# Expert weights in 16 KB runs over nine places, and the last two experts as one unit with a split tail

## The chip, the cores and the metric

The kernel runs on one core of a Trainium2 chip. The metric is device microseconds of one execution, the median of several runs. The kernel before takes 1447.01 us (three runs, 1445.4 to 1449.87). TensorE is called PE in the profile, VectorE DVE, ScalarE ACT, GpSimd POOL and SyncE SP.

## The reference

One layer over 256 latent and 256 context tokens of width 1024. A first part (modulated norm, a wide input projection, a bidirectional mLSTM, differential attention, gates, an output projection) gives the stream x of 256 x 1024. The change lies in what follows:

```
logits = u @ router_w + router_b                 # 256 tokens, 32 experts
top_val, top_idx = top_k(logits, 4); gate = softmax(top_val)
per expert e:   h   = u[tok] @ w1[e] + b1[e]                     # w1[e]: 1024 x 2048, 8 MiB
                act = min(h_glu,7) * sigmoid(1.702 min(h_glu,7)) * (clip(h_lin,-7,7) + 1)
                y   = act @ w2[e] + b2[e]                        # w2[e]: 1024 x 1024, 4 MiB
x = x + g2 * sum over the chosen experts of gate * y
out = rmsnorm(x, final_norm_g)
```

Everything is float32. The weights of the 32 experts are 384 MiB, and all of them are read in each execution.

## The kernel before, in words

**Experts.** Each expert has room for 64 tokens (CAP). Experts are worked off in pairs (loop at L1122). Tokens of a pair are picked with one-hot matmuls (`gather`, L1023), `expert` (L1051) multiplies them with the eight 1 MiB pieces of w1 (L1056), DVE and ACT make the activation (L1061 to L1065), a callback `between` does work of the neighbouring pair, four transposes and a copy give the activation transposed (L1069, L1071), and four 1 MiB pieces of w2 follow (L1078). `evac_y` (L1082) scales the result by g2, and `scatter` (L1088) adds it to x1 with four matmuls and four DVE adds. The scatter of a pair runs inside the next pair's first `between`; the last pair's scatter stands alone (L1159).

**Weights.** `epiece` (L1001) asks for the next 1 MiB piece of 128 partitions x 8 KB, in program order on SP's queue. The places are the 21 of ORDER (L36): two of a pool of their own (`spare`), four of the pool `ring` that the first part uses too, and 15 in memory that the first part frees piece by piece. A place is filled again when the matmuls that read it are done; SP waits in order, so one place that isn't free holds back all later loads.

**End.** After the last scatter stands an If (L1163) for the case that an expert has more than 64 tokens; its body is not entered with these inputs. Behind it come the final norm (sums of squares on ACT and DVE, L1201 to L1206; the reciprocal root by eight small DVE operations, L121 to L130; scaling on POOL, ACT and DVE, L1211 to L1215) and four output stores from SP (L1216).

Of the kernel before, what the change touches and what calls it, by code (L numbers as in the profile page):

```python
# [10 lines left out]
F32 = mybir.dt.float32  # L11
# [3 lines left out]
AF = mybir.ActivationFunctionType  # L15
OP = mybir.AluOpType
# [4 lines left out]
D = 1024  # L21
# [3 lines left out]
E = 32  # L25
# [1 line left out]
EPS = 1e-6  # L27
LAM_INIT = 0.2
NEG = -1.0e30
R1, R2, R3, LOOK = 4, 15, 2, 2  # L30
PER_M, PER_D = 5, 5
FAR = 4096.0

HOMES = dict(xc=[0], wk=[1, 2], mk=[3], mv=[4, 5], sums=[6, 7], hm=[8], dk=[1, 3], dv=[2, 4], og=[0], ah=[6], al=[7],
             od=[5], tg=[8, 0], bh=[1], bl=[2], yh=[3], yl=[4], wo=[6, 7])
ORDER = (-1, -1, 1, 2, 3, 9, 0, 0, 0, 0, 5, 6, 12, 4, 10, 11, 7, 8, 13, 14, 15)  # L36

B_MQ, B_MK, B_MV, B_O, B_DQ, B_DK, B_DV, B_P8, B_P9 = 0, 1, 2, 4, 6, 8, 10, 12, 14
C_G = 2048
# [66 lines left out]
def hybrid_layer(ctx: ExitStack, tc, a, out, dbg=None):  # L106
# [35 lines left out]


    keep = ctx.enter_context(tc.tile_pool(name="keep", bufs=1))
    ring = ctx.enter_context(tc.tile_pool(name="ring", bufs=R1))
    spare = ctx.enter_context(tc.tile_pool(name="spare", bufs=R3))
    dram = ctx.enter_context(tc.tile_pool(name="dram", bufs=1, space=DRAM))

    def piece(src_ap, k, n, pool_=None, tile_=None):

        w = tile_ if tile_ is not None else (pool_ or ring).tile([128, 2048], F32, name="w", tag="w")
        nc.sync.dma_start(w[:, 0:k * n], src_ap)
        return w[:, 0:k * n].rearrange("p (k n) -> p k n", k=k)

    fr = ExitStack()
    early = ctx.enter_context(tc.tile_pool(name="early", bufs=1))
    four = fr.enter_context(tc.tile_pool(name="four", bufs=3))
    tmp2 = fr.enter_context(tc.tile_pool(name="tmp2", bufs=6))
    big = [fr.enter_context(tc.tile_pool(name="big%d" % i, bufs=1)) for i in range(9)]
# [832 lines left out]


    tp = lambda name, bufs, **kw: ctx.enter_context(tc.tile_pool(name=name, bufs=bufs, reuse_waits="tile", **kw))
    ring2 = [tp("ring2_%d" % i, 1) for i in range(R2)]
    mo = tp("mo", 1)
    mt = tp("mt", 1)
    ps_m = tp("ps_m", 1, space=PSUM)
    nth = [0]

    def epiece(src, k, n):  # L1001
        i = nth[0] % (R1 + R2 + R3)
        nth[0] += 1
        return piece(src, k, n, tile_=slot(i))


    def slot(i):
        if ORDER[i] == -1:
            return spare.tile([128, 2048], F32, name="ws", tag="ws")
        if ORDER[i] == 0:  # L1010
            return ring.tile([128, 2048], F32, name="w", tag="w")
        return slot2(ORDER[i])

    def slot2(i):
        return ring2[i - 1].tile([128, 2048 + 16 * (i - 4 in HOMES["mv"])], F32, name="v%d_" % i)[:, 0:2048]

    bank1 = lambda n, bufs=1: ps_m.tile([128, 512], F32, name=n, tag=n, bufs=bufs)
    g2r = rows_[1]
# [29 lines left out]
        act.copy(PGT.rearrange("p i t -> p (i t)"), p4)  # L1048
        return PGT

    def expert(XG, sw, G, w1p, w2p, between):  # L1051

        for k in range(KT):
            w = w1p(k)
            for f in range(4):
                mm(G[f // 2][64 * (f % 2):64 * (f % 2) + 64], XG[:, k, sw * CAP:sw * CAP + CAP],  # L1056
                   w[:, f * 512:f * 512 + 512], start=False, stop=(k == KT - 1))
        g = mt.tile([128, 512], F32, name="eg")
        s = mt.tile([128, 512], F32, name="es")
        l = mt.tile([128, 512], F32, name="el")  # L1060
        dve.tensor_scalar(g, G[0], 7.0, None, op0=OP.min)  # L1061
        act.activation(s, g, AF.Sigmoid, scale=1.702)  # L1062
        dve.tensor_scalar(l, G[1], 7.0, -7.0, op0=OP.min, op1=OP.max)
        dve.scalar_tensor_tensor(l, l, 1.0, g, op0=OP.add, op1=OP.mult)
        dve.tensor_tensor(out=l, in0=l, in1=s, op=OP.mult)  # L1065
        between()
        pt_ = bank1("ptr")
        for j in range(4):
            tr(pt_[:, j * 128:j * 128 + 128], l[:, j * 128:j * 128 + 128], ident)  # L1069
        aT_ = mt.tile([128, 4, 128], F32, name="eaT")  # L1070
        act.copy(aT_.rearrange("p j s -> p (j s)"), pt_)  # L1071
        Y = bank1("py")
        for kf in range(KT):
            w = w2p(kf)
            fh, j = kf // 4, kf % 4
            for dh in range(2):
                r = 64 * (dh ^ sw)
                mm(Y[r:r + 64], aT_[:, j, fh * 64:fh * 64 + 64], w[:, dh * 512:dh * 512 + 512],  # L1078
                   start=(kf == 0), stop=(kf == KT - 1))
        return Y  # L1080
# [16 lines left out]
    def pair_in(pr):  # L1097
        P = mt.tile([128, 2, 2, CAP], F32, name="P", tag="P")
        onehots(P, posm[:, :, 2 * pr:2 * pr + 2], 2)
        return P, gated(P, gate[:, :, 2 * pr:2 * pr + 2], 2)  # L1100
# [18 lines left out]

    pend = PGT = None  # L1120
    full = (slice(0, 128), slice(0, 128))
    for pr in range(E // 2):  # L1122
        nxt = {}
        Y2 = mt.tile([128, 2, 512], F32, name="Y2")
        for sw in range(2):
            e = 2 * pr + sw
            w2c = {}

            def w1p(k):
                return epiece(a["w1"][e, k * 128:(k + 1) * 128, :], 1, 2048)[:, 0]  # L1130

            def w2p(kf):
                if kf % 2 == 0:
                    w2c[0] = epiece(a["w2"][e, kf // 2], 2, 1024)
                return w2c[0][:, kf % 2]

            def between():
                if sw == 0:
                    if pend:
                        scatter(*pend)  # L1140
                    else:
                        out_bias()
                    if pr == 0:
                        nxt["PGT0"] = transposed(PG, 2)
                    if pr + 1 < E // 2:
                        nxt["P"] = pair_in(pr + 1)
                elif pr + 1 < E // 2:
                    nxt["XG"] = gather(nxt["P"][0], 2)
                    nxt["PGT"] = transposed(nxt["P"][1], 2)

            Y = expert(XG, sw, G01[e] if e < 2 else bias_of(e), w1p, w2p, between)
            evac_y(Y2, Y, sw)
        pend = nxt["PGT0"] if pr == 0 else PGT, Y2, full
        if pr == 1:
            fng = mo.tile([128, D], F32, name="fng", tag="b2")
            nc.sync.dma_start(fng, bass.AP(tensor=a["fng"].tensor, offset=a["fng"].offset, ap=[[0, 128], [1, D]]))
        if "XG" in nxt:
            XG, PGT = nxt["XG"], nxt["PGT"]
    scatter(*pend)  # L1159


    most = nc.values_load(cnt[0:1, 0:1], min_val=0, max_val=T)
    with tc.If(most > CAP):  # L1163
# [3 lines left out]
        with tc.For_i(0, E, 1) as e:  # L1167
            pg2 = mt.tile([128, 2, 2], F32, name="pg2")
            nc.gpsimd.dma_start(pg2, scr[:, :, :, ds(e, 1)].rearrange("p i t o -> p i (t o)"))
            b1e = slot2(1)[0:1, :].rearrange("p (f n) -> p f n", f=4)  # L1170
            nc.gpsimd.dma_start(b1e, a["b1"].rearrange("(f e) n -> e f n", e=E)[ds(e, 1)])
            for r in range(1, T // CAP):
                dve.tensor_scalar(pg2[:, 0], pg2[:, 0], -float(CAP), None, op0=OP.add)
# [3 lines left out]
                PGT = transposed(gated(P, pg2[:, 1, :, None], 1), 1)  # L1177
                w2c = {}

                def w1p(k):  # L1180
                    w = slot2(2 + k % 8)
                    nc.sync.dma_start(w[:, None, :], a["w1"][ds(e, 1), k * 128:(k + 1) * 128, :].rearrange("o p n -> p o n"))
                    return w

                def w2p(kf):
                    if kf % 2 == 0:
                        w = slot2(10 + kf // 2)
                        nc.sync.dma_start(w[:, None, :], a["w2"][ds(e, 1), kf // 2].rearrange("o p n -> p o n"))
                        w2c[0] = w.rearrange("p (k n) -> p k n", k=2)
                    return w2c[0][:, kf % 2]  # L1190

                Y = expert(XG, 0, biased(lambda f: (ones[0:1, 0:CAP], b1e[:, f])), w1p, w2p, lambda: None)
                Y2 = mt.tile([128, 2, 512], F32, name="Y2")
                evac_y(Y2, Y, 0)
                scatter(PGT, Y2, (slice(0, 64), slice(64, 128)))


    ssf = mt.tile([128, 2, 2], F32, name="ssf")
    parts = [(tt, dh, slice(dh * 512, dh * 512 + 512)) for tt in range(2) for dh in range(2)]
    for tt, dh, s in parts:  # L1200
        j = mt.tile([128, 512], F32, name="el" if tt else "es")  # L1201
        if tt:
            dve.scalar_tensor_tensor(j, x1[:, tt, s], 1.0, x1[:, tt, s], op0=OP.mult, op1=OP.mult,  # L1203
                                     accum_out=ssf[:, tt, dh:dh + 1])
        else:
            act.activation(j, x1[:, tt, s], AF.Square, accum_out=ssf[:, tt, dh:dh + 1])  # L1206
    sft = mt.tile([128, 2], F32, name="sft")
    dve.tensor_tensor(out=sft, in0=ssf[:, :, 0], in1=ssf[:, :, 1], op=OP.add)  # L1208
    rsf = rstd_of(mt, sft, D, [128, 2], "rsf")
    for tt, dh, s in parts:  # L1210
        if dh == 0:  # L1211
            pool.tensor_tensor(out=x1[:, tt, s], in0=x1[:, tt, s], in1=fng[:, s], op=OP.mult)
            act.activation(x1[:, tt, s], x1[:, tt, s], AF.Copy, scale=rsf[:, tt:tt + 1])
        else:
            dve.scalar_tensor_tensor(x1[:, tt, s], x1[:, tt, s], rsf[:, tt:tt + 1], fng[:, s], op0=OP.mult, op1=OP.mult)  # L1215
        nc.sync.dma_start(out[tt * 128:(tt + 1) * 128, s], x1[:, tt, s])  # L1216


def layout(i):
# [38 lines left out]
    r["w_o"] = blocks(f(i["w_out"]).reshape(D, D))  # L1258
    r["rw"] = f(f(i["router_w"]).reshape(KT, 128, E).transpose(1, 0, 2))
    r["rb"] = f(i["router_b"]).reshape(1, E)  # L1260
    r["w1"] = f(i["exp_w1"]).reshape(E, D, 2 * D)
    r["b1"] = f(f(i["exp_b1"]).reshape(E, 4, 512).transpose(1, 0, 2)).reshape(128, 512)
    r["w2"] = rows(f(i["exp_w2"]).reshape(E * D, D), 2).reshape(E, 4, 128, 2 * D)
    r["b2"] = f(i["exp_b2"]).reshape(E, D)
    r["fng"] = f(i["final_norm_g"]).reshape(D)
    return r
# [16 lines left out]
```

## Time and profile before

| | |
|---|---|
| median of three runs | 1447.01 us |
| profiled execution: its own time | 1449.34 us |
| its span, first to last instruction | 1447.5 us |
| PE busy | 1339.6 us (93%) |
| DVE, ACT, POOL busy | 539.0, 273.6, 47.4 us |
| moved by DMA | 483.89 MB, of it 480.36 MB on SP's queue |
| granted TensorE clock, mean | 0.988 |

The span falls into the first part (to about 503 us), the experts (503 to 1436 us) and the final norm with the stores (1436 to 1447.5 us). In the 40 slices of the profile each digit is a busy share in tenths, so a stage with another limit shows as a change along the line. A wait in square brackets names the idle time of the engine before the instruction and what ended it.

### The profile page before, as it was taken

The page shows a single profiled execution, that of the slowest core. Times are in us where ns is not written, and L with a number is a line of the kernel's source. Part 1 is how long each engine was busy: PE and PEld are TensorE (multiplying, and loading weights), DVE is VectorE, ACT ScalarE, POOL GpSimd, SP SyncE. Part 2 cuts the span into 40 slices and gives each one's busy share as a digit, 9 for nine tenths or more (in the row PEclk, how much of TensorE's full clock was granted, in tenths as well). Part 3 has the DMA queues.
Part 4 walks back from the last instruction along what each step waited for, and adds up shares of the span by engine and source line. Part 5 has one row for each costly group of instructions (what it writes and reads, how often), then busy time and mean ns, then how long its engine had stood idle before and what let it go on. Part 6 is the DMA issues. An engine that isn't in the chain of part 4 may idle for free. (4 is left out here: it accounts for less than half of the span.)

```text
span 1447.5 us, 17225 instructions
## 1 busy us (share of the span) xinstructions
PE 1339.6 (93%) x6981; PEld 715.6 (49%) x6981; DVE 539.0 (37%) x1040; ACT 273.6 (19%) x569; POOL 47.4 (3%) x62
## 2 busy tenths in 40 slices
PE   5999989999998999999999999999999999999995
PEld 4778767778987633433433333343333332333331
DVE  3586764786667621221221221221212212122113
ACT  3433334445643300000000000000000000000001
POOL 0030001000020000000000000000000000000000
PEclk9999999999999989999999999999999999999998
DMA  8566343123459789999999999999999999999993
GB/s 344 207 250 237 133 166 115 61 90 116 148 221 421 284 336 421 421 420 421 420 422 420 422 420 421 420 422 420 421 421 422 420 422 421 422 420 421 421 421 141
DMA packets 68832, 483.89 MB, mean 334 GB/s; under 512 B 8387, under 2 KB 8644, under 8 KB 10636
## 3 DMA queue, kind: packets, MB, share of 16 engines
q1 hardware_dynamic: 67948, 480.36, 81.7%
q0 software_dynamic: 800, 2.38, 0.4%
q8 instruction: 57, 0.93, 0.3%
q14 instruction: 27, 0.22, 0.0%
HBM read 481.64 MB, written 1.06 MB: 333 GB/s over the span
## 5 line engine op out<-in xcount | busy, mean ns | idle before, releaser
L1061 DVE TENSOR_SCALAR eg<-acc 128x512 f32<-128x512 f32 x32 | 22.1, 692 | 443.4 <-PE acc L1056 443.4
L1062 ACT ACTIVATE es<-eg 128x512 f32<-128x512 f32 x32 | 20.2, 630 | 722.6 <-DVE eg L1061 722.6
L1086 DVE TENSOR_TENSOR Y<-py,g2r 64x512 f32<-64x512 f32 x64 | 44.1, 689 | 278.0 <-PE py L1078 277.3
L560 DVE TENSOR_TENSOR wl<-w,wh 128x512 fp32r<-128x512 f32 (+1 forms) x160 | 109.4, 692 | 83.3 <-ACT wh L559 78.4
L583 PE MATMUL acc<-uh,wh 128*128 128x256 f32 (+1 forms) x328 | 108.1, 330 | 0.9 <-ACT wh L559 0.9
L559 ACT CAST wh<-w 128x512 fp32r<-128x512 f32 (+1 forms) x160 | 93.4, 603 | 62.4 <-PE acc L575 24.6
L585 PE MATMUL acc<-uh,wl 128*128 128x256 f32 (+1 forms) x328 | 103.6, 316 | 0.4 <-DVE wl L560 0.4
L584 PE MATMUL acc<-ul,wh 128*128 128x256 f32 (+1 forms) x328 | 103.5, 316 | 0.0
L1056 PE MATMUL acc<-w,XG 128*64 128x512 f32 x400 | 90.5, 595 | 3.3 <-DMA w<-in_w_dram 3.3
L583 PEld LDWEIGHTS acc<-uh,wh 128*128 128x128 f32 x328 | 62.1, 189 | 13.0 <-ACT wh L559 4.2
L573 PE MATMUL acc<-wh,uh 128*128 128x512 f32 x160 | 64.7, 404 | 1.0 <-DVE gi L341 0.7
L1030 PEld LDWEIGHTS pga<-P,u 128*128 128x128 f32 x512 | 58.4, 192 | 12.5 <-DVE eg L1061 12.2
L585 PEld LDWEIGHTS acc<-uh,wl 128*128 128x128 f32 x328 | 61.7, 188 | 5.6 <-DVE wl L560 0.8
L584 PEld LDWEIGHTS acc<-ul,wh 128*128 128x128 f32 x328 | 61.9, 189 | 4.3 <-DVE ul L287 0.3
L575 PE MATMUL acc<-wh,ul 128*128 128x512 f32 x160 | 62.9, 393 | 0.0
L574 PE MATMUL acc<-wl,uh 128*128 128x512 f32 x160 | 62.8, 393 | 0.1
L1030 PE MATMUL pga<-P,u 128*128 128x128 f32 x512 | 61.4, 278 | 0.3 <-DVE P L941 0.3
L804 PE MATMUL acc<-b1s,cst 128*64 128x512 f32 x256 | 60.2, 592 | 0.0
L1092 PE MATMUL acc<-Y,PGT 128*128 128x512 f32 x128 | 59.2, 605 | 0.8 <-DVE Y L1086 0.8
L1056 PEld LDWEIGHTS acc<-w,XG 128*64 128x64 f32 x400 | 27.8, 137 | 63.2 <-issue 49.4
L1056 PE MATMUL acc<-ws,XG 128*64 128x512 f32 x224 | 51.0, 594 | 1.8 <-SPq L1163 1.2
L1078 PE MATMUL py<-w,eaT 128*64 128x512 f32 x176 | 41.5, 619 | 3.6 <-ACT eaT L1071 3.6
(876 smaller groups left out, 2008.8 us busy)
## 6 DMA issues: line engine op xcount, KB each, us to landing
w<-in_w_dram SPq DMA_DIRECT2D x72, 1024.0 KB, 19.8
ws<-in_w_dram SPq DMA_DIRECT2D x38, 1024.0 KB, 19.8
w<-in_w_in_dram SPq DMA_DIRECT2D x30, 1024.0 KB, 4.9
w<-in_ada_w_dram SPq DMA_DIRECT2D x24, 1024.0 KB, 5.0
w<-in_w_a_dram SPq DMA_DIRECT2D x4, 1024.0 KB, 5.7
wo<-in_w_o_dram SPq DMA_DIRECT2D x4, 1024.0 KB, 7.1
w<-in_w_b_dram SPq DMA_DIRECT2D x4, 1024.0 KB, 10.8
wk<-in_w_in_dram SPq DMA_DIRECT2D x2, 1024.0 KB, 13.7
```

What stands on the lines that cost most here:

```text
L559: act.copy(wh[:, 0:n], raw)
L560: dve.tensor_tensor(out=wl[:, 0:n], in0=raw, in1=lanes(wh[:, 0:n]), op=OP.subtract)
L573: mm(self.ps[j], vh[:, k, s], wh, start=st, stop=False)
L574: mm(self.ps[j], vh[:, k, s], wl, start=False, stop=False)
L575: mm(self.ps[j], vl[:, k, s], wh, start=False, stop=sp)
L583: mm(o, wh[:, c], vh[:, k, t0:t1], start=f, stop=False, skip_group_check=g)
L584: mm(o, wh[:, c], vl[:, k, t0:t1], start=False, stop=False, skip_group_check=g)
L585: mm(o, wl[:, c], vh[:, k, t0:t1], start=False, stop=sp, skip_group_check=g)
L804: mm(G[f // 2][64 * (f % 2):64 * (f % 2) + 64], *bias(f), start=True, stop=False)
L1030: mm(p[:, kk, 0:n * CAP], u2[:, tt, k * 128:k * 128 + 128], P[:, tt].rearrange("p e s -> p (e s)"), start=(tt == 0), stop=(tt == 1))
L1056: mm(G[f // 2][64 * (f % 2):64 * (f % 2) + 64], XG[:, k, sw * CAP:sw * CAP + CAP], w[:, f * 512:f * 512 + 512], start=False, stop=(k == KT ...
L1092: mm(p, PGT[parts[dh], 2 * dh + tt, :], Y2[parts[dh], dh], start=True, stop=True)
```

## The change

Four things are changed.

1. The expert weights are laid out so that one load takes 2 MiB, 128 partitions x 16 KB: w1 in four loads per expert, w2 in two. ORDER now names eleven fillings of 2 MiB, one of them in two separate 8 KB places (9 and 12) and one half in place 15 and half in `s`; behind these, nine 16 KB places are used in turn (AGAIN). The pool `ring` becomes part of the memory that the first part gives back; its four places are A and B.
2. The last two experts are a unit of their own: both do w1 and the activation first; then w2 of both is loaded by column halves (2 KB runs, 512 columns), and the two experts' products go to the two halves of the partitions of one PSUM bank. The left 512 columns of x are finished before the right ones.
3. The final norm is split: squares and the product with the norm's weights for the left columns follow the left half's scatter; the rest follows the right half's. The outputs go out by two DMA queues, SP's and ACT's.
4. Norm and stores stand ahead of the If; in its body they are done again.

```diff
-R1, R2, R3, LOOK = 4, 15, 2, 2
-ORDER = (-1, -1, 1, 2, 3, 9, 0, 0, 0, 0, 5, 6, 12, 4, 10, 11, 7, 8, 13, 14, 15)
+PLACES = (("A", 2, 0), ("B", 2, 0), (1, 2, 0), (3, 2, 0), (5, 2, 0), (7, 2, 1), (9, 1, 1), (10, 2, 0), (12, 1, 0),
+          (13, 2, 0), (15, 1, 0))
+ORDER = ("s", 1, "A", "B", 5, (9, 12), 3, 10, 7, 13, (15, "s"))
+AGAIN = (1, "A", "B", 5, 3, 10, 7, 13, "s")
...
+    def slot(i):
+        if i == "s":
+            return spare.tile([128, 4096], F32, name="ws", tag="ws")
+        pool_, n, pad = ring2[i]
+        return pool_.tile([128, 2048 * n + 16 * pad], F32, name="v%s_" % i)[:, 0:2048 * n]
+    def epiece(src=None):
+        i = nth[0]
+        nth[0] += 1
+        where = ORDER[i] if i < len(ORDER) else AGAIN[(i - len(ORDER)) % len(AGAIN)]
+        if isinstance(where, tuple):
+            h = [slot(w)[:, 0:2048] for w in where]
+            for n in range(2):
+                nc.sync.dma_start(h[n], src[:, n * 2048:(n + 1) * 2048])
+            return h
+        w = slot(where)
+        if src is not None:
+            nc.sync.dma_start(w, src)
+        return [w[:, 0:2048], w[:, 2048:4096]]
...
+    aTs = []
+    for sw in range(2):
+        e = E - 2 + sw
+        aTs.append(hidden(XG, sw, bias_of(e), w1_of(e), (lambda: None) if sw else (lambda: scatter(*pend)),
+                          slot(9)[:, 0:512].rearrange("p (j s) -> p j s", j=4) if sw else None))
+    Y2 = mt.tile([128, 2, 512], F32, name="Y2")
+    for dh in range(2):
+        s = slice(dh * 512, dh * 512 + 512)
+        Y = bank1("pga", 2)
+        for fh in range(2):
+            w = [v.rearrange("p (k n) -> p k n", k=4) for v in epiece()]
+            step = 2 if dh and fh else 4
+            for k0 in range(0, 4, step):
+                for i in range(2):
+                    src = a["w2"][E - 2 + i, fh].rearrange("p (k n) -> p k n", k=4)
+                    nc.sync.dma_start(w[i][:, k0:k0 + step], src[:, k0:k0 + step, s])
+            for j in range(4):
+                for i in range(2):
+                    mm(Y[64 * i:64 * i + 64], aTs[i][:, j, fh * 64:fh * 64 + 64], w[i][:, j],
+                       start=(fh == 0 and j == 0), stop=(fh == 1 and j == 3))
+        dve.tensor_tensor(out=Y2[:, dh], in0=Y, in1=g2r[:, s], op=OP.mult)
+        for tt in range(2):
+            p = acc()
+            mm(p, PGT[:, tt, :], Y2[:, dh], start=True, stop=True)
+            dve.tensor_tensor(out=x1[:, tt, s], in0=x1[:, tt, s], in1=p, op=OP.add)
+        norm_part(dh)
+    norm_end()
...
+    def norm_part(dh):
+        s = slice(dh * 512, dh * 512 + 512)
+        for tt in range(2):
+            j = mt.tile([128, 512], F32, name="es")
+            act.activation(j, x1[:, tt, s], AF.Square, accum_out=ssf[:, dh, tt:tt + 1])
+        if dh == 0:
+            for tt in range(2):
+                dve.tensor_tensor(out=xo[:, tt, 0], in0=x1[:, tt, s], in1=fng[:, s], op=OP.mult)
+            dve.tensor_scalar(rsf[0], ssf[:, 0], 1.0 / D, EPS, op0=OP.mult, op1=OP.add)
+    def norm_end():
+        v, y, t = rsf
+        dve.scalar_tensor_tensor(v, ssf[:, 1], 1.0 / D, v, op0=OP.mult, op1=OP.add)
+        rsqrt(y, v, t)
+        for tt in range(2):
+            rows_of = out[tt * 128:(tt + 1) * 128]
+            act.activation(xo[:, tt, 0], xo[:, tt, 0], AF.Copy, scale=y[:, tt:tt + 1])
+            nc.scalar.dma_start(rows_of[:, 0:512], xo[:, tt, 0])
+            dve.scalar_tensor_tensor(xo[:, tt, 1], x1[:, tt, 512:1024], y[:, tt:tt + 1], fng[:, 512:1024],
+                                     op0=OP.mult, op1=OP.mult)
+            nc.sync.dma_start(rows_of[:, 512:1024], xo[:, tt, 1])
...
-    r["w1"] = f(i["exp_w1"]).reshape(E, D, 2 * D)
+    r["w1"] = rows(f(i["exp_w1"]).reshape(E * D, 2 * D), 2).reshape(E, 4, 128, 4 * D)
-    r["w2"] = rows(f(i["exp_w2"]).reshape(E * D, D), 2).reshape(E, 4, 128, 2 * D)
+    r["w2"] = rows(f(i["exp_w2"]).reshape(E * D, D), 4).reshape(E, 2, 128, 4 * D)
```

`hidden` is the first half of `expert`, up to and with the transposed activation; `w1_of(e)` hands out the two 8 KB halves of each 16 KB load of w1 as the pieces of its eight steps.

## Rows read from the trace of the kernel before

**Rows 1.** The page: busy time of PE; DMA share in 40 slices.
```profile
PE 1339.6 (93%) x6981; PEld 715.6 (49%) x6981; DVE 539.0 (37%) x1040; ACT 273.6 (19%) x569; POOL 47.4 (3%) x62
...
DMA  8566343123459789999999999999999999999993
```

**Rows 2.** Three stretches: length, busy by engine, clock, DMA share, GB/s.
```profile
527.00:533.00 6.00, 5.33 (x16) 1.54 (x16) 0.04 (x1) 0.58 (x1) 0.29 (x1) 0.58 0.11 16
533.00:567.00 34.00, 32.54 (x170) 13.50 (x168) 6.12 (x9) 2.29 (x4) 0.00 (x0) 1.00 1.00 412
567.00:1410.00 843.00, 798.17 (x3796) 304.67 (x3794) 175.16 (x276) 50.27 (x86) 4.11 (x14) 1.00 1.01 421
```

**Rows 3.** DMA queues, 567 to 1410 us: packets, MB, share of 16 engines.
```profile
DMA packets 48751, 354.77 MB, mean 421 GB/s; under 512 B 5413, under 2 KB 5413, under 8 KB 5541
...
q1 hardware_dynamic: 48710, 354.19, 101.1%
q8 instruction: 30, 0.49, 0.2%
```

**Rows 4.** DMA queues, 1442 to 1447.5 us: the output stores, 2 KB runs.
```profile
DMA packets 576, 1.05 MB, mean 191 GB/s; under 512 B 64, under 2 KB 64, under 8 KB 576
...
q1 hardware_dynamic: 576, 1.05, 49.6%
```

**Rows 5.** Timeline in a late expert: start, us, engine, line [idle before].
```profile
1384.57 1.94 PE L1056 MATMUL acc<-v__8357,XG 128*64 128x512 f32 x8 [0.55 <-DMA v__8357<-in_w_dram]
1384.59 0.33 SPq L152 DMA_DIRECT2D v__8441<-in_w_dram  x1
```

**Rows 6.** Timeline, first experts: SP's issues and PE.
```profile
432.32 1.01 SPq L152 DMA_DIRECT2D ws<-in_w_dram  x2
...
501.81 0.33 SPq L152 DMA_DIRECT2D v__4948<-in_w_dram  x1
...
515.14 18.87 SPq L152 DMA_DIRECT2D w<-in_w_dram  x4
...
528.01 5.63 PE L1078 MATMUL py<-w,eaT 128*64 128x512 f32 x16 [0.67 <-ACT eaT L1071]
...
536.90 1.88 PE L1056 MATMUL acc<-v__4856,XG 128*64 128x512 f32 x8
...
540.55 0.33 SPq L152 DMA_DIRECT2D v__5074<-in_w_dram  x1
...
560.82 2.04 SPq L152 DMA_DIRECT2D ws<-in_w_dram  x2
```

**Rows 7.** Timeline of the end, from the last piece of w1 on.
```profile
1414.53 1.94 PE L1056 MATMUL acc<-ws,XG 128*64 128x512 f32 x8 [0.69 <-SPq L1163]
...
1420.23 3.68 PE L1078 MATMUL py<-v__8487,eaT 128*64 128x512 f32 x8 [0.73 <-ACT eaT L1071]
...
1426.72 1.88 PE L1078 MATMUL py<-v__8499,eaT 128*64 128x512 f32 x8
1428.44 1.88 PE L1078 MATMUL py<-v__8505,eaT 128*64 128x512 f32 x8
...
1431.12 3.70 PE L1092 MATMUL acc<-Y,PGT 128*128 128x512 f32 x8 [0.80 <-DVE Y L1086]
...
1433.14 0.69 DVE L1094 TENSOR_TENSOR x<-x,acc 128x512 f32<-128x512 f32 x1 [0.17 <-PE acc L1092]
...
1436.60 0.63 ACT L1206 ACTIVATE es<-x 128x512 f32<-128x512 f32 x1
...
1439.90 0.17 DVE L122 TENSOR_SCALAR rsfy<-rsfv 128x2 int32<-128x2 int32 x1
...
1441.54 1.33 ACT L1213 ACTIVATE x<-x,rsfy 128x512 f32<-128x512 f32 x2 [4.22 <-DVE rsfy L130]
```

**Rows 8.** One stretch of the end, columns as in rows 2.
```profile
1419.50:1426.30 6.80, 6.07 (x17) 1.75 (x18) 0.00 (x0) 0.58 (x1) 0.00 (x0) 0.50 0.31 128
```

**Rows 9.** The stores' line: durations in ns min/median/max, first and last start.
```profile
L1216 SPq DMA_DIRECT2D out_dram<-x x4: 351/380/405, 1442.3 to 1443.7; - x4
```

More of the change, by code (lines that the diff above doesn't have):

```diff
@@ L29 @@
 NEG = -1.0e30
-R1, R2, R3, LOOK = 4, 15, 2, 2
+R1, LOOK = 4, 2
 PER_M, PER_D = 5, 5
@@ L144, in hybrid_layer @@
     keep = ctx.enter_context(tc.tile_pool(name="keep", bufs=1))
-    ring = ctx.enter_context(tc.tile_pool(name="ring", bufs=R1))
-    spare = ctx.enter_context(tc.tile_pool(name="spare", bufs=R3))
+    early = ctx.enter_context(tc.tile_pool(name="early", bufs=1))
+    spare = ctx.enter_context(tc.tile_pool(name="spare", bufs=1))
+    fr = ExitStack()
+    ring = fr.enter_context(tc.tile_pool(name="ring", bufs=R1))
     dram = ctx.enter_context(tc.tile_pool(name="dram", bufs=1, space=DRAM))
@@ L153, in piece @@
         return w[:, 0:k * n].rearrange("p (k n) -> p k n", k=k)
-    fr = ExitStack()
-    early = ctx.enter_context(tc.tile_pool(name="early", bufs=1))
     four = fr.enter_context(tc.tile_pool(name="four", bufs=3))
@@ L994, in hybrid_layer @@
     tp = lambda name, bufs, **kw: ctx.enter_context(tc.tile_pool(name=name, bufs=bufs, reuse_waits="tile", **kw))
-    ring2 = [tp("ring2_%d" % i, 1) for i in range(R2)]
+    ring2 = {i: (tp("ring2_%s" % i, 1), n, pad) for i, n, pad in PLACES}
     mo = tp("mo", 1)
@@ L999, in hybrid_layer @@
     nth = [0]
-    def epiece(src, k, n):
-        i = nth[0] % (R1 + R2 + R3)
-        nth[0] += 1
[L1004 to L1015, printed above, removed]
+    def slot(i):
[5 more added lines that the diff above has]
+        i = nth[0]
+        nth[0] += 1
+        where = ORDER[i] if i < len(ORDER) else AGAIN[(i - len(ORDER)) % len(AGAIN)]
[8 more added lines that the diff above has]
+        return [w[:, 0:2048], w[:, 2048:4096]]
     bank1 = lambda n, bufs=1: ps_m.tile([128, 512], F32, name=n, tag=n, bufs=bufs)
@@ L1049, in transposed, with hidden @@
         return PGT
-    def expert(XG, sw, G, w1p, w2p, between):
+    def hidden(XG, sw, G, w1p, between, aT_=None):
         for k in range(KT):
@@ L1069, in expert @@
             tr(pt_[:, j * 128:j * 128 + 128], l[:, j * 128:j * 128 + 128], ident)
-        aT_ = mt.tile([128, 4, 128], F32, name="eaT")
+        if aT_ is None:
+            aT_ = mt.tile([128, 4, 128], F32, name="eaT")
         act.copy(aT_.rearrange("p j s -> p (j s)"), pt_)
+        return aT_
+    def expert(XG, sw, G, w1p, w2p, between):
+        aT_ = hidden(XG, sw, G, w1p, between)
         Y = bank1("py")
@@ L1121, in hybrid_layer, with w1_of, w1p @@
     full = (slice(0, 128), slice(0, 128))
-    for pr in range(E // 2):
+    def w1_of(e):
+        got = {}
+        def w1p(k):
+            if k % 2 == 0:
+                got[0] = epiece(a["w1"][e, k // 2])
+            return got[0][k % 2]
+        return w1p
+    for pr in range(E // 2 - 1):
         nxt = {}
@@ L1127, in hybrid_layer @@
             w2c = {}
-            def w1p(k):
-                return epiece(a["w1"][e, k * 128:(k + 1) * 128, :], 1, 2048)[:, 0]
             def w2p(kf):
-                if kf % 2 == 0:
-                    w2c[0] = epiece(a["w2"][e, kf // 2], 2, 1024)
-                return w2c[0][:, kf % 2]
+                if kf % 4 == 0:
+                    w2c[0] = epiece(a["w2"][e, kf // 4])
+                return w2c[0][kf % 4 // 2].rearrange("p (k n) -> p k n", k=2)[:, kf % 2]
             def between():
@@ L1144, in between @@
                         nxt["PGT0"] = transposed(PG, 2)
-                    if pr + 1 < E // 2:
-                        nxt["P"] = pair_in(pr + 1)
-                elif pr + 1 < E // 2:
+                    nxt["P"] = pair_in(pr + 1)
+                else:
                     nxt["XG"] = gather(nxt["P"][0], 2)
                     nxt["PGT"] = transposed(nxt["P"][1], 2)
-            Y = expert(XG, sw, G01[e] if e < 2 else bias_of(e), w1p, w2p, between)
+            Y = expert(XG, sw, G01[e] if e < 2 else bias_of(e), w1_of(e), w2p, between)
             evac_y(Y2, Y, sw)
@@ L1156, in hybrid_layer @@
             nc.sync.dma_start(fng, bass.AP(tensor=a["fng"].tensor, offset=a["fng"].offset, ap=[[0, 128], [1, D]]))
-        if "XG" in nxt:
-            XG, PGT = nxt["XG"], nxt["PGT"]
-    scatter(*pend)
+        XG, PGT = nxt["XG"], nxt["PGT"]
+    xo = slot(12).rearrange("p (t h n) -> p t h n", t=2, h=2)
+    ssf = mt.tile([128, 2, 2], F32, name="ssf")
+    rsf = [mt.tile([128, 2], F32, name="rsf" + n) for n in "vyt"]
+    def norm_part(dh):
[7 more added lines that the diff above has]
+            dve.tensor_scalar(rsf[0], ssf[:, 0], 1.0 / D, EPS, op0=OP.mult, op1=OP.add)
@@ L1169, in hybrid_layer @@
             nc.gpsimd.dma_start(pg2, scr[:, :, :, ds(e, 1)].rearrange("p i t o -> p i (t o)"))
-            b1e = slot2(1)[0:1, :].rearrange("p (f n) -> p f n", f=4)
+            b1e = slot(15)[0:1, :].rearrange("p (f n) -> p f n", f=4)
             nc.gpsimd.dma_start(b1e, a["b1"].rearrange("(f e) n -> e f n", e=E)[ds(e, 1)])
@@ L1178, in hybrid_layer, with any_piece @@
                 w2c = {}
+                def any_piece(src, i):
+                    w = slot(i)
+                    nc.sync.dma_start(w[:, None, :], src.rearrange("o p n -> p o n"))
+                    return w
                 def w1p(k):
-                    w = slot2(2 + k % 8)
-                    nc.sync.dma_start(w[:, None, :], a["w1"][ds(e, 1), k * 128:(k + 1) * 128, :].rearrange("o p n -> p o n"))
-                    return w
+                    if k % 2 == 0:
+                        w2c[1] = any_piece(a["w1"][ds(e, 1), k // 2], ("s", "A", "B", 1)[k // 2])
+                    return w2c[1][:, k % 2 * 2048:k % 2 * 2048 + 2048]
                 def w2p(kf):
[L1186 to L1190, printed above, removed]
+                    if kf % 4 == 0:
+                        w2c[0] = any_piece(a["w2"][ds(e, 1), kf // 4], (5, 7)[kf // 4])
+                    return w2c[0][:, kf % 4 * 1024:kf % 4 * 1024 + 1024]
                 Y = expert(XG, 0, biased(lambda f: (ones[0:1, 0:CAP], b1e[:, f])), w1p, w2p, lambda: None)
@@ L1195, in hybrid_layer @@
                 scatter(PGT, Y2, (slice(0, 64), slice(64, 128)))
[L1198 to L1216, printed above, removed]
+        for dh in range(2):
+            norm_part(dh)
+        norm_end()
 def layout(i):
```

## The prediction, made before the changed kernel ran

> **What bounds the kernel now.** The page comes first: PE is busy for 93% of the span, but the DMA line holds at 9 from the middle to the end [rows 1]. Two limits are close, so the stage of the experts must show which one waits. The stretches do: from 567 to 1410 us the 16 DMA engines are recorded busy for 1.01 of the time at 421 GB/s [rows 2]. The timeline of a late expert settles it: PE starts on a piece of w1 after 0.55 us of idle time, ended by that piece's landing, and SP issues the next load 0.02 us behind that landing [rows 5]. So the stream of weights is the bound, PE follows it, and what counts is when the stream starts without holes, how fast it runs, and what is left after its last piece. SP's queue carries 354.19 MB in those 843 us [rows 3], 420.1 GB/s or 2.496 us for each MiB of 1.0486 MB.
>
> Durations are those of the profiled execution (its own time 1449.3 us, span 1447.5); the median of the runs is 2.3 us lower. I add the sum of the changes to both alike.
>
> **Part 1a, the places: a loss at the start.** Before, SP issues 21 pieces from 432.32 to 501.81 us and eight more up to 517 us (the first two of the four of 515.14 among them) [rows 6]. These 29 MiB have landed at 527 us. Then DMA is nearly idle (16 GB/s) until 533 us, since the next place is read by w2 of the first expert; from 533 to 567 us it moves 34 x 412 GB/s = 14.0 MB, 13.4 MiB [rows 2]. So 42.4 MiB are in at 567 us.
>
> With the new order the first eleven fillings are 22 MiB, and 1, A and B follow, free as w1 of the first expert is read: 28 MiB. The next load wants place 5, the first half of w2, which PE reads from 528.01 for 5.63 us [rows 6]. It goes out near 533.7 us; with 1.2 us to its first bytes (an estimate: the stream restarts near 533 us, some 1.2 us after the first piece of that w2 is read) and 4.9 us for 2 MiB it is in at 539.8. The places 9 and 12 aren't filled again, so the next load waits for place 3, the first two pieces of the second expert's w1: read from 536.90 [rows 6] for 2 x 1.72 us (the step from 1426.72 to 1428.44 us for a 1 MiB piece [rows 7]), SP free at 540.55 [rows 6], in at 546.7. The places 10, 7 and 13 come free every 3.44 us and keep DMA busy: 36 MiB at 556.5, 38 at 561.4. Place s is free at 560.82 [rows 6]: 40 MiB at 566.9. From there, five more places come free in w1 steps and hold 24.6 us of traffic, longer than PE's pause between w1 and w2, so no hole follows. At 567 us 40.0 stand against 42.4 MiB: **+6.0 us** (2.4 x 2.496).
>
> **Part 1b, 16 KB runs: a gain in pace.** No row has a weight packet of 16 KB. From the shares: SP's queue takes 1.011 x 16 x 843 = 13,636 us for 48,710 packets, of which 5,413 are tiny and 128 are under 8 KB [rows 3]; counted on the 43,169 large ones that is 315.4 ns for 8 KB, tiny ones included. The stores' 512 runs of 2 KB with their 64 tiny ones take 0.496 x 16 x 5.5 = 43.6 us [rows 4], 85.2 ns each. The line through both has 38.37 ns per KB and 8.5 ns per packet. So 16 KB would take 622.4 ns against 630.8 for two of 8 KB: 1.33%, 0.0332 us per MiB. Over the 336 MiB from the 40th to the 376th (the last of w1) that is **-11.2 us**, the value I take. Other ends: the records overlap by 1.1%, so 3.4 of the 8.5 ns may be hidden already; 5.1 ns halved over 312 ns is 0.82%, -6.9 us. Nothing at all, if the engines are held by bytes or split the runs. Below nothing: instruction packets of 16 KB take 0.2% of 13,488 us for 30, 0.9 us each [rows 3]; they go elsewhere than weights, so the 8 KB row on the same queue is nearer.
>
> A rule speaks for less. The rows give 8.5 ns per packet by the line. The Trainium skill, "DMA: Bandwidth & Descriptors", section "Why small descriptors are slow (HBM only)", puts the fixed cost at about three bus cycles a packet beside one per 32 bytes. By it 8 KB is 259 cycles and 16 KB saves 1.5 of them per 8 KB, 0.58%: an estimate of -4.9 us instead of -11.2.
>
> PE now waits for 2 MiB: some 1.5 us idle per 4.9 us. This costs nothing while the stream is the bound. If the clock fell in such waits, a 2 MiB step would take 6.9 us, PE would fall behind, its waits would go and the clock return; at most some 3 us stay at the end.
>
> **Parts 2 and 3, the end.** Before, the last piece of w1 lands at 1414.5 us [rows 7] with 380 MiB ahead of w2, and 33.0 us follow. Now w2 of expert 30 comes behind, so the last of w1 is reached with 376 MiB: **-10.0 us**. What follows grows. From that landing: w1 step 1.72, then the last piece as before, 1420.23 - 1414.53 = 5.70, together 7.42. First 2 MiB of w2: 6.49 us, as the first two pieces took from 1420.23 to 1426.72 [rows 7] at a granted clock of 0.50, the 1.2 GHz level, after PE had waited for the activation [rows 8]. Second 2 MiB: 3.44. Left half: 0.80 for its scaling [rows 7] and 1.7 for two matmuls. Two more of 2 MiB: 6.9. That is 26.7 us. Then the right half: from the end of w2 (1430.16) to the end of the second add (1433.83) 3.7 [rows 7]; the square 0.63 [rows 7] and 0.3 for hand-over and sum (an estimate); 0.2 and eight small operations, 1439.90 to 1441.48, 1.6; ACT's two scalings with a store issue between them, 1.8 [rows 7, 9]; from the last store's issue at 1443.7 to the end 3.8 [rows 9]. With 0.5 for the If behind the stores (between 0 and the 0.7 of a wait at it, rows 7) that is 12.5, together 39.2: **+6.3 us** over 33.0 (unrounded terms).
>
> Hidden: the 2 KB runs, 256 per engine at 85.2 ns, 21.8 us for 8 MiB, plus 1.7 for the last matmuls, are done 3.2 us before PE. SP must describe 512 runs per MiB; a store of 128 took 0.38 us [rows 9], so 1.5 us against 2.7 us of traffic. The left half's scaling, squares and products on DVE and ACT lie beside the 6.9 us of the right half's w2. Behind SP's stores nothing waits but the If.
>
> Sum: 6.0 - 11.2 - 10.0 + 6.3 = **-8.9 us**: 1440.4 for the profiled execution, 1438.1 for the median.
>
> **Rivals.**
> No gain in pace, because the stream is held by bytes: for it speaks the 1.01 share, against it the 8.5 ns. The sum is then +2.3 us, 1449.3. A smaller fixed cost: if only 3.7 of the 8.5 ns are real and the rest is overlap, 3.7 halved over 312 ns is 0.59%, -4.9 us, and the sum is -2.6, 1444.4. The overlapping records speak for it, the line through the two sizes against it. The rule above gives the same.
> A slower stream: if a 16 KB packet takes more than 632 ns (two of 8 KB and 0.23%, 1.9 us over 838.7 us of stream), the sum passes +4.3 us, slower. The place is the whole stretch to the last w1. At 2% slower it is 2.3 + 16.8 = +19 us, 1466. For it speaks the 0.9 us of the instruction packets, against it that 2 KB and 8 KB lie on a line with a positive start.
> A better end: if PE keeps 2.4 GHz through w2, the first 2 MiB take 3.44 instead of 6.49 us: 1435.0. PE's 5.7 us without w1 or w2 work are there as before, which speaks against it.
>
> **Numbers.** About 0.3%, 4.3 us, is what can be told from no change here. Forecast with a gain of 6.9 us or more: 0.50. Better end: 0.10. Bytes as the bound, or no effect of the runs: 0.13; the smaller fixed cost: 0.12. Slower stream: 0.15. Faster 0.60, same 0.25, slower 0.15. The range runs from 1431 (a better end and some luck in pace) to 1450 (no gain in pace); the slower stream and a little below stay out.
>
> **What would show it.** 16 KB packets near 622 ns in the stretch 600 to 1390 us, and about 426 GB/s there; a hole of DMA from about 525 to 535 and a short one near 541 us; the last of w1 landing near 1400 us and some 39 us behind it; a granted clock of 0.50 at the first half of the left w2. It is wrong if the pace stays at 420 GB/s, if the holes before 567 us are absent, or if w2's 2 KB runs land after PE could use them.

## The result, and the profile after

The changed kernel takes 1439.14 us (median of six runs, 1437.74 to 1443.55) against 1448.27 us for the kernel before on the same chips (six runs): ratio 0.9945, 95% interval 0.9927 to 0.9963, some 8 us less (5 to 11). The forecast was -8.9 us. The profiled execution took 1442.55 us, span 1440.8; it is the second longest of the six, 3.4 us above the median, so below it is distances inside one execution that are compared.

The first block is the page of the changed kernel, to be held against [rows 1]; the second has stretches of it, in the columns of [rows 2].

```profile
PE 1338.4 (93%) x6981; PEld 720.3 (50%) x6981; DVE 534.3 (37%) x1036; ACT 275.3 (19%) x573; POOL 44.6 (3%) x60
...
DMA  8566343123469679999999999999999999999994
```

```profile
520.00:527.00 7.00, 6.33 (x12) 2.25 (x11) 5.87 (x9) 0.59 (x1) 0.00 (x0) 0.54 0.93 396
527.00:533.00 6.00, 5.32 (x16) 1.84 (x18) 0.42 (x1) 0.59 (x1) 0.29 (x1) 0.50 0.01 5
533.00:567.00 34.00, 32.54 (x168) 13.46 (x166) 6.05 (x9) 2.29 (x4) 0.00 (x0) 0.98 0.87 346
600.00:1390.00 790.00, 747.15 (x3584) 290.43 (x3582) 166.42 (x262) 49.08 (x84) 3.84 (x13) 1.00 1.01 428
```

The DMA engines are busy without a break in the long stretch, now at 428 instead of 421 GB/s; before 567 us the stream lost ground, 346 GB/s where it had 412. The queues from 600 to 1390 us, to be held against [rows 3]:

```profile
DMA packets 23197, 337.76 MB, mean 428 GB/s; under 512 B 2579, under 2 KB 2579, under 8 KB 2579
...
q1 hardware_dynamic: 23161, 337.23, 100.4%
```

That is 20,582 packets of 16 KB at 616.6 ns (1.004 x 16 x 790 us, the tiny ones included; the forecast was 622.4) and 337.23 MB in 790 us, 2.456 us per MiB.

How much PE waits for this stream is in the next lines: what it waited for from 600 to 1390 us (us in total, times, longest; the first of 17 lines for landings), and its first wait for a landing in the changed kernel and in the kernel before (start, duration).

```profile
PE py L1095 <- ACT eaT L1083: 19.7, 27, 0.7
PE ptr L1080 <- ACT PGT L1059: 10.2, 14, 0.7
PE acc L1067 <- DMA v__7437<-in_w_dram: 1.3, 1, 1.3
...
1055.41 3.65 PE L1067 MATMUL acc<-v__6795,XG 128*64 128x512 f32 x16 [0.93 <-DMA v__6795<-in_w_dram]
...
1084.75 1.94 PE L1056 MATMUL acc<-v__7167,XG 128*64 128x512 f32 x8 [0.55 <-DMA v__7167<-in_w_dram]
```

The 17 waits for a landing come to 12.8 us; PE's work and its waits for ACT fill the rest of the 790 us. Until 1055 us PE lives on the lead with which the stream began, although DMA is saturated all the while; only from there on does it wait, some three times per pair of experts. So the stream sets when the kernel ends, but by a margin of some 13 us.

SP's issues and PE in the first experts, to be held against [rows 6] (start, duration):

```profile
517.08 0.33 SPq L1025 DMA_DIRECT2D vB__4960<-in_w_dram  x1
...
528.67 6.37 PE L1095 MATMUL py<-v__4811,eaT 128*64 128x512 f32 x16 [0.68 <-ACT eaT L1083]
...
535.08 0.33 SPq L1025 DMA_DIRECT2D v__4970<-in_w_dram  x1
541.95 0.33 SPq L1025 DMA_DIRECT2D v__4980<-in_w_dram  x1
```

SP stands still for 18 us: the load into place 5 waits until PE has read the first 2 MiB of w2, the next for place 3. The end, to be held against [rows 7], and behind it stretches of it, the first against [rows 8]:

```profile
1400.81 3.65 PE L1067 MATMUL acc<-v__8056,XG 128*64 128x512 f32 x16
...
1407.37 1.39 PE L1227 MATMUL pga<-v__8082,eaT 128*64 128x512 f32 x2
...
1412.55 0.59 PE L1227 MATMUL pga<-v__8093,eaT 128*64 128x512 f32 x1
...
1417.59 1.98 PE L1232 MATMUL acc<-Y,PGT 128*128 128x512 f32 x4 [0.78 <-DVE Y L1229]
...
1427.39 1.99 PE L1232 MATMUL acc<-Y,PGT 128*128 128x512 f32 x4 [0.79 <-DVE Y L1229]
...
1434.67 0.34 ACTq L1203 DMA_DIRECT2D out_dram<-v__7941  x1
```

```profile
1408.00:1411.40 3.40, 3.40 (x10) 1.90 (x10) 0.00 (x0) 0.06 (x1) 0.00 (x0) 0.50 1.05 390
1411.40:1431.00 19.60, 16.40 (x64) 6.31 (x60) 5.47 (x10) 2.89 (x8) 0.00 (x0) 1.00 0.37 136
1420.00:1430.00 10.00, 8.58 (x36) 2.68 (x32) 3.55 (x7) 1.65 (x6) 0.00 (x0) 1.00 0.04 13
```

From the last w1 to the end are 40.0 us (39.2 forecast). The left half of w2 starts at the clock's lower level, for 3.4 us instead of the 6.8 before. The right half follows without a wait for weights. The store by ACT starts at 1434.67, 6.1 us ahead of the end, where 3.8 us stood in [rows 9].

### The profile page after: what moved, and what is told of

It is laid out like the page before. It is cut to its first block, busy times and chain, and to the rows that moved or that the text cites. A ratio compares the mean times of both kernels' runs of the same rounds, so it can differ in the third digit from the quotient of the medians.

```text
span 1440.8 us, 16847 instructions
## 1 busy us (share of the span) xinstructions
PE 1338.4 (93%) x6981; PEld 720.3 (50%) x6981; DVE 534.3 (37%) x1036; ACT 275.3 (19%) x573; POOL 44.6 (3%) x60
## 4 chain that ended last, share of the span: by engine, by line
PE 70%; DMA 18%; DVE 5%; ACT 4%; issue 1%; SPq 0%; ACTq 0%; DVEq 0%
PE acc L1067 20%; PE py L1095 12%; PE pga L1041 4%; PE acc L588 4%; PE acc L590 4%; PE acc L589 4%; PE acc L809 3%; DMA v__7865<-in_w_dram 3%; DMA vA__7009<-in_w_dram 3%; DMA vA__7651<-in_w_dram 3%; DMA v__7223<-in_w_dram 3%; DMA v__7437<-in_w_dram 3%; DMA v__8056<-in_w_dram 2%; PE acc L578 2%; PE acc L579 2%; PE acc L580 2%
## 5 line engine op out<-in xcount | busy, mean ns | idle before, releaser
L1109 PE MATMUL acc<-Y,PGT 128*128 128x512 f32 x120 | 55.5, 605 | 0.0
L309 DVE SCALAR_TENSOR_TENSOR sums<-w,sil,sums 128x512 f32<-128x512 f32 x56 | 42.5, 775 | 0.0
L1095 PE MATMUL py<-ws,eaT 128*64 128x512 f32 x152 | 34.8, 598 | 6.6 <-ACT eaT L1083 6.6
L1067 PE MATMUL acc<-ws,XG 128*64 128x512 f32 x176 | 39.7, 593 | 0.0
L1109 PEld LDWEIGHTS acc<-Y,PGT 128*128 128x128 f32 x120 | 21.6, 189 | 33.7 <-issue 21.5
```

## The experiments

Ratios are to the kernel before on the same chip, with 95% intervals; a hundredth of a per cent is 0.14 us. The forecast has three terms, start, pace and end. Runs take out the pace and the end; no run puts the old places back, so the start is what these two leave.

**Two loads of 8 KB runs.** Places, order and end stay as changed.

```diff
-            nc.sync.dma_start(w, src)
+            for n in range(2):
+                nc.sync.dma_start(w[:, n * 2048:(n + 1) * 2048], src[:, n * 2048:(n + 1) * 2048])
```

> The changed kernel with each 2 MiB load of weights sent as two loads of 1 MiB with 8 KB runs, into the same places in the same order. Theory (a fixed cost per packet, about 9.8 ns of which show in the pace: 2.496 us per MiB at 8 KB and 2.456 at 16 KB): the pace goes back to 2.496, 420 GB/s, and the time rises by 336 x 0.039 = 13 us, to about 1452. Rival (the gain came from the places and their order, or the engines are held by bytes): the pace stays near 427 GB/s and the time near 1439.

Measured: 1450.05 us, ratio 1.0021 (1.0009 to 1.0033). Its queue, 600 to 1390 us:

```profile
DMA packets 45639, 332.60 MB, mean 421 GB/s; under 512 B 5068, under 2 KB 5068, under 8 KB 5068
...
q1 hardware_dynamic: 45604, 332.09, 101.1%
```

332.09 MB in 790 us are 2.494 us per MiB. The pace is back where it was, and without it the change is 0.1 to 0.3% slower than the kernel before.

**One load of 8 KB runs.** A load of 2 MiB stays one load, but in memory a gap of 256 bytes follows every 8 KB (RUN is 2048 numbers of 4 bytes). The w2 of the last two experts is read from a copy without gaps.

```diff
-            nc.sync.dma_start(w, src)
+            nc.sync.dma_start(w.rearrange("p (r n) -> p r n", n=RUN), src[:, :, 0:RUN])
...
+    apart = lambda v: f(np.pad(v.reshape(v.shape[:3] + (RUNS, RUN)), ((0, 0),) * 4 + ((0, 64),)))
```

> The changed kernel with each 2 MiB load still one load, but its source rows cut in two by gaps of 256 bytes in the weights' layout, so that it moves 256 runs of 8 KB. Theory (cost per packet): as with two loads, 420 GB/s, about 1452 us. Rival (cost per load, its start and its completion, of which there are half as many): the pace stays near 427 GB/s, about 1439 us. Another rival, cost per load and per packet in equal parts: about 1445.

Measured: 1451.92 us, ratio 1.0044 (1.0027 to 1.0061).

```profile
DMA packets 43109, 332.65 MB, mean 421 GB/s; under 512 B 2530, under 2 KB 2530, under 8 KB 2530
...
q1 hardware_dynamic: 43075, 332.15, 101.1%
```

The same pace with half as many loads, and so with 2,530 tiny packets (under 512 bytes) instead of 5,068. So it is the length of the run, not the number of loads.

**One load of 4 KB runs.** The same with a gap after every 4 KB.

> The same with gaps after every 4 KB. Theory: four packets of 4 KB cost 3 x 9.8 ns more than one of 16 KB, so 2.456 + 12 x 0.0098 = 2.574 us per MiB, 407 GB/s, and 336 x 0.118 = 40 us more, about 1479. Rival (8 KB and 16 KB differ by something else than their number, as the place in memory): no more than at 8 KB, about 1452.

Measured: 1476.3 us (two runs), ratio 1.0202 (1.0179 to 1.0224).

```profile
DMA packets 81267, 323.16 MB, mean 409 GB/s; under 512 B 2462, under 2 KB 2462, under 8 KB 81233
...
q1 hardware_dynamic: 81233, 322.66, 102.4%
```

2.567 us per MiB. Each engine takes 16 packets of 4 KB, 8 of 8 KB or 4 of 16 KB for a MiB: 0.073 us for eight packets more is 9.1 ns each, 0.038 us for four more is 9.5 ns. One fixed cost per packet fits all three sizes.

The recorded durations say more. By the shares (times 16 x 790 us, over the packets that aren't tiny) a packet is recorded for 164.3, 315.2 and 616.6 ns at 4, 8 and 16 KB, while an engine takes the next one after 160.5, 311.8 and 614.1 ns. Neighbouring records overlap, so the two prices differ: recorded, one packet more costs 13 to 14 ns (twice 164.3 less 315.2, twice 315.2 less 616.6), of which some 9 show in the pace and some 4 are hidden in the overlap.

**The old end.** All 16 pairs in one loop, then scatter, If, norm and stores as before; places and runs as changed.

```diff
-    for pr in range(E // 2 - 1):
+    for pr in range(E // 2):
...
-    for sw in range(2):
-        e = E - 2 + sw
...
-        norm_part(dh)
-    norm_end()
...
+    scatter(*pend)
...
```

> The changed kernel with the end of the kernel before: all 16 pairs in one loop, w2 of the last expert in 16 KB runs, scatter, If, whole norm, stores from SP alone. Theory (places, pace and end add up; the end was worth 10.0 x 0.984 - 7.0 = 2.8 us in the profiled run and 3.7 by the prediction): 1442 to 1443 us, last w1 landing about 10 us later than in the changed kernel and some 33 to 35 us behind it. Rival (the end carries the gain): 1446 or more. Rival (the new end is worth nothing): 1439.

Measured: 1443.46 us, ratio 0.9976 (0.9966 to 0.9986). The end of its profiled execution (span 1440.3 us) has the last w1 at

```profile
1406.90 3.65 PE L1067 MATMUL acc<-v__8074,XG 128*64 128x512 f32 x16 [1.24 <-SPq L1185]
```

33.4 us ahead of its end. The new end is worth 0.9976 - 0.9945 = 0.0031, about 4.5 us (with both intervals, 1.5 to 7.5).

**Places 9 and 12 once more.** One more turn is written into ORDER, with them:

```diff
-ORDER = ("s", 1, "A", "B", 5, (9, 12), 3, 10, 7, 13, (15, "s"))
+ORDER = ("s", 1, "A", "B", 5, (9, 12), 3, 10, 7, 13, (15, "s"), 1, "A", "B", 5, (9, 12), 3, 10, 7, 13, "s")
```

> The changed kernel with the places 9 and 12 filled once more, in the first turn behind the eleven fillings, so that the second half of the first expert's w2 gives 2 MiB back as well. Theory (holes in the stream before 567 us are never won back, since the stream is the bound from there on): the short hole near 542 us and those up to 562 us go, about 1.5 MiB more are in at 567 us, and the time falls by 3 to 4 us, ratio to the kernel before about 0.992. Rival (PE sets the pace of the first experts and later slack swallows the holes): no change, 0.9945.

Measured: 1436.55 us, ratio 0.9923 (0.9902 to 0.9943). Behind the hole SP now issues every 1.7 us at first:

```profile
535.58 0.33 SPq L1025 DMA_DIRECT2D v__4970<-in_w_dram  x1
537.29 0.33 SPq L1021 DMA_DIRECT2D v__4980<-in_w_dram  x1
539.01 0.33 SPq L1021 DMA_DIRECT2D v__4981<-in_w_dram  x1
```

and 374 GB/s instead of 346 are moved from 533 to 567 us. The time moved the way the theory has it, but its interval overlaps that of the changed kernel, so the time alone doesn't show it.

**Half of a scatter in the last pause.**

```diff
-        aTs.append(hidden(XG, sw, bias_of(e), w1_of(e), (lambda: None) if sw else (lambda: scatter(*pend)),
+        aTs.append(hidden(XG, sw, bias_of(e), w1_of(e), lambda: scatter(*pend, halves=(sw,)),
```

> The changed kernel with half of the scatter of pair 14 (two matmuls, two adds) moved from expert 30's pause into expert 31's. Theory (PE's wait for the last activation makes the clock fall to 0.50 for one 3.4 us stretch in the first w2 of the end, 1.7 us; with 1.7 us of matmuls in that wait it may stay): if the clock stays at 1.0 behind the last w1, 1 to 2 us less, ratio about 0.9935; the moved adds stand behind the activation's operations on DVE and cost nothing. Rival (the wait that is left is still long enough): the clock falls all the same, 0.9945.

Measured: 1436.19 us, ratio 0.9933 (0.9912 to 0.9954). The first line is the end's start in the run above, without this edit, the second in this one:

```profile
1395.00:1410.00 15.00, 12.69 (x61) 5.17 (x59) 2.76 (x4) 1.22 (x2) 0.00 (x0) 1.00 1.03 384
...
1395.00:1410.00 15.00, 13.81 (x57) 5.27 (x53) 4.65 (x7) 1.22 (x2) 0.00 (x0) 1.00 1.04 383
```

No verdict: the clock stayed at 1.00 here, but it did so without the edit too, and the interval overlaps that of the changed kernel.

**The output bias later.** The pause is PE's time between w1 and w2 of one expert, in which `between` runs. The first expert's holds four matmuls and eight DVE operations (with two transposes and a copy ahead of them) for the output bias of all experts; they go to the pause of expert 8.

```diff
-                    else:
+                    if pr == 4:
                         out_bias()
...
-        if pr == 1:
+        if pr == 5:
...
```

> The changed kernel with the experts' output bias (four matmuls and eight DVE operations in the first expert's pause) moved to the pause of expert 8, the load of the final norm's weights behind it. Theory (place 5 comes free only when the first w2 is read, and that is some 12 us behind w1 because of the bias and the low clock that follows): the pause falls to about 6 us, the hole of 9 us from 527 us on shrinks to 3 or 4, and 4 to 6 us are won: ratio about 0.991; at expert 8 the stream has enough queued. Rival (the clock and the pause stay as they are): 0.9945.

Measured: 1429.29 us, ratio 0.9877 (0.9858 to 0.9896), about 10 us under the changed kernel (6 to 14 by both intervals), where 4 to 6 were expected. PE, SP and the stretches as above:

```profile
518.50 5.03 PE L1095 MATMUL py<-v__4787,eaT 128*64 128x512 f32 x16 [0.68 <-ACT eaT L1083]
...
523.58 0.33 SPq L1025 DMA_DIRECT2D v__4946<-in_w_dram  x1
```

```profile
520.00:527.00 7.00, 7.00 (x32) 2.30 (x30) 0.00 (x0) 0.00 (x0) 0.00 (x0) 0.91 0.92 349
527.00:533.00 6.00, 6.00 (x30) 1.96 (x28) 1.38 (x2) 0.00 (x0) 0.00 (x0) 1.00 0.77 281
533.00:567.00 34.00, 32.54 (x170) 13.51 (x168) 4.75 (x7) 2.29 (x4) 0.00 (x0) 1.00 0.99 416
```

The low clock is shorter too, as one window over both pauses shows, the changed kernel first, this run behind it:

```profile
505.00:545.00 40.00, 36.79 (x140) 12.39 (x136) 10.44 (x16) 3.34 (x5) 0.29 (x1) 0.83 0.74 288
...
505.00:545.00 40.00, 37.06 (x185) 14.79 (x180) 8.28 (x13) 4.10 (x7) 0.29 (x1) 0.96 0.96 389
```

So place 5 is issued at 523.58 instead of 535.08 (2.6 us of that stood already at the end of the first w1, which the edit doesn't touch). SP's standstill falls from 18 to 9 us, and the hole of 9 us shrinks to some 3 us by the GB/s that are missing to 427 from 520 to 533 us.

**The three edits together.**

> The three edits together (places 9 and 12 filled once more, half of the scatter in expert 31's pause, bias at expert 8). Theory: the two at the start win 6 to 8 us together, the one at the end 0 to 2: about 1432 us, ratio 0.9885 to 0.990. Rival (holes at the start are swallowed later): 0.994.

Measured: 1427.32 us, ratio 0.9864 (0.9846 to 0.9881), the best version, some 20 us under the kernel before. From 527 us on the stream runs through (from 520 to 527 us it moves 353 GB/s):

```profile
527.00:533.00 6.00, 6.00 (x30) 1.97 (x28) 1.38 (x2) 0.00 (x0) 0.00 (x0) 1.00 0.98 410
533.00:567.00 34.00, 32.54 (x170) 13.50 (x168) 4.75 (x7) 2.29 (x4) 0.00 (x0) 1.00 1.01 430
```

**Norm and stores behind the If.** Norm and stores as a whole go behind the If. The unit, the column halves, the norm's operations and the two store queues stay, so the run tests the order and the early left half, not the queues.

```diff
-        norm_part(dh)
-    norm_end()
...
+    for dh in range(2):
+        norm_part(dh)
+    norm_end()
```

> The changed kernel with the whole final norm, both halves, and the stores behind the If. Theory (in the profiled run 6.1 us stood between the last store's issue and the end, 3.8 in the kernel before, because SP and ACT load the If's condition and walk through its waits behind the stores; so the order ahead of the If gives 2.3 us back of what it saves): ahead of the norm 0.6 us for the If and some 1.6 us for two more squares, behind the stores 2.3 us less: the time stays within 1 us of the changed kernel, ratio about 0.9945. Rival (stores ahead of the If are worth what they hide, 2 us and more): 0.996 or more.

Measured: 1438.74 us, ratio 0.9932 (0.9915 to 0.9948). Norm and stores ahead of the If show no gain; by both intervals one of 1.5 us would still fit. The last store here goes out 4.15 us ahead of the end (span 1436.8):

```profile
1432.65 0.34 ACTq L1203 DMA_DIRECT2D out_dram<-v__7941  x1
```

**The bias later in the kernel before.** The edit of `out_bias` and `fng` alone.

> The kernel before with the experts' output bias moved to the pause of expert 8, all else as it is. Theory (the pause of the first expert holds the places, so that the stream stands still from 527 to 533 us, and the rest of the stream can't win it back): the hole of 5 us goes, ratio 0.996 to 0.9965. Rival (with 21 small places the stream has slack here that the changed kernel hasn't): 1.000.

Measured: 1440.1 us, ratio 0.9941 (0.9924 to 0.9958), some 8 us (6 to 11), more than the 5 expected. The hole of [rows 2] is gone:

```profile
527.00:533.00 6.00, 6.00 (x32) 2.00 (x30) 1.38 (x2) 0.00 (x0) 0.00 (x0) 1.00 1.02 425
533.00:567.00 34.00, 32.54 (x172) 13.55 (x170) 4.74 (x7) 2.29 (x4) 0.00 (x0) 1.00 1.01 420
```

As far as the intervals tell, moving these few small operations is worth as much as the whole change.

## Why the prediction was right, step by step

- **The bound.** Right for the sum, with less room than it reads. DMA is saturated from 567 us on, but PE first waits for a landing at 1055 us (1085 us in the kernel before). It has caught up with the stream well before the last w1, so time follows bytes and pace. Holes filled before 567 us then come back at the end: with the bias moved 3.7 MB more are in from 520 to 567 us in the changed kernel, 8.7 us at 427 GB/s (6 to 14 measured), and 2.7 MB more from 527 to 567 us in the kernel before, 6.5 us at 420 GB/s (6 to 11 measured).
- **Start, +6.0.** Right in its places: 28 MiB, then a hole until place 5 is read, a short one at place 3. By the runs it is what pace and end leave, (1.0021 - 1) + 0.0031 = 0.0052, about 7.5 us (4 to 11). The profiled execution has 28 + 11.2 MiB (34 x 346 GB/s) at 567 us against the 42.4 of before: 3.2 MiB, 8.0 us. Some 1.4 of the 2 us above the forecast are there because place 5 went out at 535.08 instead of 533.7 us: PE read the first w2 a little later and slower (528.67 for 6.37 us, against 528.01 for 5.63 in [rows 6]). That the two executions are so close here is luck; in those of the runs above whose code is the same up to there, PE starts on it between 522.59 and 529.04 us.
- **Pace, -11.2.** The mechanism, a cost per packet, was right; that the size came out so near is partly luck. Measured are 1.0021 - 0.9945 = 0.0076, 11 us (8 to 14); the profiled stretches alone give 336 x (2.496 - 2.456) = 13.4. The forecast took 8.5 ns per packet, from a line through the 2 KB stores, and let none of it hide. On the weights' own queue a packet costs 13 to 14 ns by the records; some 4 of them are hidden in overlap (the lower bound supposed 3.4) and 9.1 to 9.5 show. So the line was some 5 ns short, the overlap left out was some 4, and the two nearly cancelled. The rule of the Trainium skill ("DMA: Bandwidth & Descriptors", section "Why small descriptors are slow (HBM only)") puts the fixed cost at about three cycles a packet, an estimate of 4.9 us in the prediction. The runs do not agree with it at these sizes: 11 us (8 to 14) were measured.
- **PE's longer waits.** Right that they cost nothing: the clock stays at 1.00 from 600 to 1390 us. Wrong that there are many: not 1.5 us idle per 4.9 us, but 17 waits of 0.3 to 1.3 us, 12.8 us in all, where the kernel before has 24 and 12.9 us in the same stretch. PE reads a 2 MiB piece in 3.44 us, but the rest of its work, that the prediction left out here, takes up nearly all the time between.
- **End, -10.0 and +6.3.** The sum, -3.7, met 4.5 (1.5 to 7.5). Its terms were off against each other. The last w1 to w2 took 6.56 instead of 7.42 us, and the first 2 MiB 5.2 instead of 6.49, as the low clock was shorter. From the second 2 MiB to the left half's scatter it took 5.04 (1412.55 to 1417.59) instead of 4.24 us. The If behind the stores, costed at 0.5, took some 2 us: 6.1 us from the last store to the end, 4.15 with the If ahead of them. That is the mis-sized term. As much as the early norm saves, the If seems to take back, which fits the run with the norm behind the If; then the gain of the end lies in part 2 or in the second store queue, which no run takes apart. That it is the loading of the If's condition and SP's walk through its waits is argued, not shown.
- **2 KB runs.** Right that they stay hidden: DMA moves 13 GB/s from 1420 to 1430 us, and no matmul of the right half waits for weights.
- **Rivals.** Bytes as the bound fell with the 8 KB and 4 KB runs; the smaller fixed cost, -4.9 us, with the 8 to 14 us measured; a slower stream with the 616.6 ns. The better end did not come in the profiled execution (0.50 from 1408.0 to 1411.4 us), though it did in the one with places 9 and 12 once more, whose end is the same.

What stays open: whether the matmuls put into the last pause hold the clock, since it held without them too; and the start by a run of its own.

## What to carry to other kernels

Where DMA is saturated, count its packets: run length was a gain of its own here. Two stretches of one profile with different run lengths give a first estimate of the price of a packet (8.5 ns here), but records overlap; what counts is the price in the pace (9.1 to 9.5 ns), which takes a run with another run length. Before making a stream faster still, sum up what the other engine waits for it: some 13 us were left here, and some 7 with the three edits, whatever the stream gains. A place that is freed by an instruction behind a long pause turns that pause into a hole in the stream; shorten the pause that stands in front of the first reuse before giving up places for longer runs. A hole cost about its full length in this kernel, because the same stream still set the end.

## What the runs showed of the hardware that was not expected

Stores ahead of the If took 3.8 to 4.0 us from issue to landing (3.4 to 4.1 in the other runs with that end), the same stores behind the If 2.8 to 3.0 us, and those from SP alone in the kernel before 2.0 to 2.4 us. What delays them is not shown. The granted clock stayed at the lower of its two levels for 10 to 14 us in the first expert's pause and behind it in the kernels with the bias there (means of 0.83 to 0.87 from 505 to 545 us), and for 3 us in the three without it (0.96); whether the small matmuls or the length of the pause do that is not taken apart.
